# Four rows per partition, spread in place and stored as one 64 KB run: an RMSNorm that repeats its rows

## The chip, the cores and the metric

The kernel runs on one core of one Trainium2 chip. The metric is the device time of one execution in microseconds; the profile is one execution on the same core.

## The reference

```python
# x: (8, 512, 2048) float32, gamma: (2048,) float32
def reference(x, gamma):
    x_rep = np.repeat(x, 2, axis=1)
    rms = np.sqrt((x_rep ** 2).mean(axis=-1, keepdims=True) + 1e-6)
    x_norm = x_rep / rms
    return (x_norm * gamma[None, None, :]).astype(np.float32)
```

Each of the 4096 rows of 2048 values is divided by its root mean square, multiplied by gamma, and written twice, one copy after the other. So 33.55 MB (4096 rows of 8 KB) are read, and 67.11 MB are written.

## The kernel before

The rows are cut into 16 tiles of 256. Each of the 128 partitions holds K = 2 neighbouring rows, so a tile's load is 2.10 MB, with 16 KB in one run for each partition.

Loads are issued from SyncE (SP) on line 59, into `x_tile`. On ACT, line 64 squares each of the two rows into `sq_tile` and sums it into one column of `ss`, and line 72 takes the root for both rows at once. On DVE, line 80 takes the reciprocals, line 84 scales each row into `y_tile` (which is `sq_tile` again), and line 87 multiplies both rows by gamma. Then POOL issues two stores on line 90, one for each repetition: each takes the same two rows, and writes them to every second row of the output, so that a run in the output is one row of 8 KB.

The pools `xin` and `sq` have six buffers each. The Tile framework sets the order of the instructions on each engine and the waits between them: a load waits until the scaling of six tiles ago has read `x_tile`, and a square waits until both stores of six tiles ago have read `sq_tile`. Gamma is loaded on line 44, ahead of all x, into one partition, and POOL spreads it over the 128 partitions on line 45.

Of the kernel before, what the change touches and what calls it, by code (L numbers as in the profile page):

```python
# [1 line left out]

# [4 lines left out]


@with_exitstack  # L10
def kernel(
    ctx: ExitStack,
    tc: tile.TileContext,
    x: bass.AP,
    gamma: bass.AP,
    out: bass.AP,
):
    nc = tc.nc
    P = nc.NUM_PARTITIONS

    B, S, D = x.shape
    Bo, So, Do = out.shape
    R = So // S
    assert D == Do and B == Bo and So == S * R
    eps = 1e-6

    x_f = x.rearrange("b s d -> (b s) d")
    N = B * S
    K = 2
    assert N % (P * K) == 0  # L30
    ntiles = N // (P * K)
    x_t = x_f.rearrange("(n p k) d -> n p k d", p=P, k=K)

    out_v = out.rearrange("b (s r) d -> (b s) r d", r=R)
    out_t = out_v.rearrange("(n p k) r d -> n p k r d", p=P, k=K)

    BUFS = 6
    singles = ctx.enter_context(tc.tile_pool(name="singles", bufs=1))
    xin = ctx.enter_context(tc.tile_pool(name="xin", bufs=BUFS))
    sq = ctx.enter_context(tc.tile_pool(name="sq", bufs=BUFS))  # L40
    small = ctx.enter_context(tc.tile_pool(name="small", bufs=8))

    gamma_b = singles.tile([P, D], mybir.dt.float32)
    nc.sync.dma_start(out=gamma_b[0:1, :], in_=gamma.partition_broadcast(1))
    nc.gpsimd.partition_broadcast(out_ap=gamma_b[:], in_ap=gamma_b[0:1, :])  # L45
    gamma_kd = bass.AP(
        tensor=gamma_b.tensor,
        offset=gamma_b.offset,
        ap=[gamma_b.ap[0], [0, K], gamma_b.ap[1]],
    )  # L50

    eps_t = singles.tile([P, 1], mybir.dt.float32)
    nc.vector.memset(eps_t, eps)  # L53

    inv_d = 1.0 / float(D)

    for i in range(ntiles):
        x_tile = xin.tile([P, K, D], mybir.dt.float32, name="x_tile")
        nc.sync.dma_start(out=x_tile[:], in_=x_t[i])

        sq_tile = sq.tile([P, K, D], mybir.dt.float32, name="sq_tile")
        ss = small.tile([P, K], mybir.dt.float32, name="ss")
        for k in range(K):
            nc.scalar.activation(  # L64
                out=sq_tile[:, k, :],
                in_=x_tile[:, k, :],
                func=mybir.ActivationFunctionType.Square,
                accum_out=ss[:, k : k + 1],
            )

        rms = small.tile([P, K], mybir.dt.float32, name="rms")
        nc.scalar.activation(  # L72
            out=rms[:],
            in_=ss[:],
            func=mybir.ActivationFunctionType.Sqrt,
            scale=inv_d,
            bias=eps_t[:],
        )
        rstd = small.tile([P, K], mybir.dt.float32, name="rstd")
        nc.vector.reciprocal(out=rstd[:], in_=rms[:])  # L80

        y_tile = sq_tile
        for k in range(K):
            nc.vector.tensor_scalar_mul(  # L84
                out=y_tile[:, k, :], in0=x_tile[:, k, :], scalar1=rstd[:, k : k + 1]
            )
        nc.vector.tensor_mul(out=y_tile[:], in0=y_tile[:], in1=gamma_kd)  # L87

        for r in range(R):
            nc.gpsimd.dma_start(out=out_t[i, :, :, r, :], in_=y_tile[:])  # L90


# [1 line left out]
_INS = ['x', 'gamma']  # L94
_OUTS = [((8, 1024, 2048), 'float32')]


# [23 lines left out]
```

## Time and profile before

| | |
|---|---|
| median of 9 runs | 245.0 us (244.92 to 245.18) |
| the profiled execution | 245.1 us, with a span of 243.2 us |
| DVE, ACT, POOL busy | 112.6, 69.5, 29.3 us |
| HBM read, written | 33.56 MB, 67.11 MB |
| store, issue to landing | 40.5 us at the median, 32 stores of 2048 KB |
| load, issue to landing | 24.5 us at the median, 16 loads of 2048 KB |

The span runs from the first instruction of the program to the last; the time of an execution has 1.9 us around it. Below, a group's row gives the line, the engine and the operation, then its busy time and the mean duration of one, and then the idle time of the engine ahead of it with what ended it. In the timeline and the chain, a row starts with its start and its duration in microseconds. The rows of the slices cut the span into 40 equal parts of 6.08 us.

### The profile page before, as it was taken

To read this page: it belongs to the slowest core of one execution; us is meant where nothing else is said; L and a number is where in the kernel's file an instruction comes from. 1 tells how busy PE (TensorE), PEld (TensorE's weight loads), DVE (VectorE), ACT (ScalarE), POOL (GpSimd) and SP (SyncE) were. 2 spreads that over 40 slices of the span, in tenths; PEclk is the share of its full clock that TensorE was granted. 3 is DMA by queue.
4 is the path that set the end of the run, shared out by engine and by line. 5 is a ranking of instruction groups with operands and counts; after the bars stand their busy time and mean duration, and the time that the engine had idled before them with its cause. 6 is when DMAs were issued, how large, how long until landed. Compare 5 with 4: busy or idle time off the path is not lost.

```text
span 243.2 us, 320 instructions
## 1 busy us (share of the span) xinstructions
DVE 112.6 (46%) x65; ACT 69.5 (29%) x82; POOL 29.3 (12%) x37
## 2 busy tenths in 40 slices
DVE  0069999950900049690095709587595600000000
ACT  2598666006000150600615060642624000000000
POOL 4003223411010101110120111111121111000000
DMA  6999999999999999999999999999999999999993
GB/s 220 431 431 431 406 427 430 433 425 431 426 427 435 427 423 429 431 439 422 426 429 438 415 429 430 427 429 429 429 420 425 416 420 419 426 419 425 418 425 148
DMA packets 11012, 100.69 MB, mean 414 GB/s; under 512 B 769, under 2 KB 769, under 8 KB 769
## 3 DMA queue, kind: packets, MB, share of 16 engines
q0 software_dynamic: 8704, 67.11, 65.6%
q1 hardware_dynamic: 2306, 33.56, 32.8%
q14 instruction: 2, 0.02, 0.0%
HBM read 33.56 MB, written 67.11 MB: 414 GB/s over the span
## 4 chain that ended last, share of the span: by engine, by line
DMA 50%; another core or an unknown queue 15%; issue 4%; ACT 3%; DVE 2%; POOL 1%; POOLq 0%; ACTq 0%
DMA out_dram<-sq_tile 50%; ACT sq_tile L64 3%; DVE sq_tile L87 2%; POOL out_dram L90 1%; POOLq L116 0%; ACT rms L72 0%; DVE rstd L80 0%; ACTq L64 0%; POOLq L90 0%
## 5 line engine op out<-in xcount | busy, mean ns | idle before, releaser
L64 ACT ACTIVATE sq_tile<-x_tile 128x2048 f32<-128x2048 f32 x32 | 60.8, 1901 | 114.4 <-DMA out_dram<-sq_tile 101.2
L87 DVE TENSOR_TENSOR sq_tile<-sq_tile,gamma_b 128x4096 f32<-128x4096 f32 x16 | 70.8, 4422 | 0.5
L90 POOL DMA_DIRECT2D out_dram<-sq_tile x32 | 26.8, 839 | 170.3 <-DMA out_dram<-sq_tile 126.6
L84 DVE TENSOR_SCALAR sq_tile<-x_tile,rstd 128x2048 f32<-128x2048 f32 x32 | 40.0, 1293 | 0.5
L80 DVE RECIPROCAL rstd<-rms 128x2 f32<-128x2 f32 x16 | 2.6, 163 | 78.1 <-ACT rms L72 78.1
L64 ACT ACTIVATION_READ_ACCUMULATOR sq_tile<-x_tile 128x1 f32 x32 | 6.0, 186 | 0.0
L72 ACT ACTIVATE rms<-ss,eps_t 128x2 f32<-128x2 f32 x16 | 4.7, 295 | 0.5
L45 POOL PARTITION_BROADCAST gamma_b<-gamma_b x1 | 2.3, 2293 | 2.2 <-DMA gamma_b<-in_gamma_dram 2.2
L64 ACT ACT_TABLE_LOAD x1 | 1.3, 1283 | 0.7 <-PEq L105 0.7
L72 ACT ACT_TABLE_LOAD x1 | 1.3, 1283 | 0.0
L53 DVE MEMSET eps_t<- 128x1 f32 x1 | 0.1, 59 | 0.8 <-PEq L105 0.8
L105 POOL MEMSET const-float32-0.0<- 128x1 f32 x1 | 0.1, 100 | 0.2 <-issue 0.2
L105 POOL MEMSET const-bfloat16-1.0<- 128x1 bf16 x1 | 0.1, 102 | 0.0
L105 POOL MEMSET const-uint8-127<- 128x1 uint8 x1 | 0.1, 102 | 0.0
L105 POOL MEMSET const-float32-1.0<- 128x1 f32 x1 | 0.1, 98 | 0.0
## 6 DMA issues: line engine op xcount, KB each, us to landing
out_dram<-sq_tile POOLq DMA_DIRECT2D x32, 2048.0 KB, 40.5
x_tile<-in_x_dram SPq DMA_DIRECT2D x16, 2048.0 KB, 24.5
gamma_b<-in_gamma_dram SPq DMA_DIRECT2D x1, 8.0 KB
```

The lines of the kernel that those rows point to most:

```text
L45: nc.gpsimd.partition_broadcast(out_ap=gamma_b[:], in_ap=gamma_b[0:1, :])
L53: nc.vector.memset(eps_t, eps)
L64: nc.scalar.activation(out=sq_tile[:, k, :], in_=x_tile[:, k, :], func=mybir.ActivationFunctionType.Square, accum_out=ss[:, k : k + 1],)
L72: nc.scalar.activation(out=rms[:], in_=ss[:], func=mybir.ActivationFunctionType.Sqrt, scale=inv_d, bias=eps_t[:],)
L80: nc.vector.reciprocal(out=rstd[:], in_=rms[:])
L84: nc.vector.tensor_scalar_mul(out=y_tile[:, k, :], in0=x_tile[:, k, :], scalar1=rstd[:, k : k + 1])
L87: nc.vector.tensor_mul(out=y_tile[:], in0=y_tile[:], in1=gamma_kd)
L90: nc.gpsimd.dma_start(out=out_t[i, :, :, r, :], in_=y_tile[:])
L105: nc = _bacc.Bacc("TRN2", target_bir_lowering=False, num_devices=1)
```

## The change

A tile now has K = 4 rows per partition, so there are 8 tiles. Input and output share one buffer `y` of eight rows (64 KB per partition), of which there are three. A load of 4.19 MB puts the four rows of x into the last four slots. Row k of x, in slot 4 + k, is scaled and multiplied by gamma in one DVE instruction into slot 2k, and copied from there to slot 2k + 1: by ACT for the first three rows, and by DVE for the fourth, whose second copy lands on the row of x itself. When all eight slots are filled, ACT issues one store of 8.39 MB, in which each partition is one run of 64 KB. The squares go to a PSUM tile that nobody reads; only their sum is used.

Loads 0 to 2 are issued from SP at the start, the first in four parts of one row each; later loads are issued from SP when their buffer is free. Gamma's load is issued from ACT.

```diff
-    K = 2
+    K = 4
...
-    out_t = out_v.rearrange("(n p k) r d -> n p k r d", p=P, k=K)
+    out_t = out.rearrange("b s d -> (b s) d").rearrange("(n p j) d -> n p (j d)", p=P, j=K * R)
...
-    BUFS = 6
-    xin = ctx.enter_context(tc.tile_pool(name="xin", bufs=BUFS))
-    sq = ctx.enter_context(tc.tile_pool(name="sq", bufs=BUFS))
+    rows = ctx.enter_context(tc.tile_pool(name="rows", bufs=3))
+    junk = ctx.enter_context(tc.tile_pool(name="junk", bufs=1, space=bass.MemoryType.PSUM))
...
+    def load(i, parts=1):
+        y = rows.tile([P, K * R, D], f32, name="y")
+        step = K // parts
+        for k in range(0, K, step):
+            at = K * (R - 1) + k
+            nc.sync.dma_start(out=y[:, at : at + step, :], in_=x_t[i, :, k : k + step, :])
+        ys.append(y)
+    load(0, parts=K)
...
-    nc.sync.dma_start(out=gamma_b[0:1, :], in_=gamma.partition_broadcast(1))
+    nc.scalar.dma_start(out=gamma_b[0:1, :], in_=gamma.partition_broadcast(1))
...
+    load(1)
+    load(2)
...
     for i in range(ntiles):
+        y = ys[i]
         for k in range(K):
+            xk = y[:, K * (R - 1) + k, :]
+            y0, y1 = y[:, R * k, :], y[:, R * k + 1, :]
+            sq = junk.tile([P, D], f32, name="sq")
+            ss = small.tile([P, 1], f32, name="ss")
+            nc.scalar.activation(out=sq[:], in_=xk, func=Act.Square, accum_out=ss[:])
+            rms = small.tile([P, 1], f32, name="rms")
+            nc.scalar.activation(out=rms[:], in_=ss[:], func=Act.Sqrt, scale=inv_d, bias=eps_t[:])
+            rstd = small.tile([P, 1], f32, name="rstd")
+            nc.vector.reciprocal(out=rstd[:], in_=rms[:])
+            nc.vector.scalar_tensor_tensor(
+                out=y0, in0=xk, scalar=rstd[:], in1=gamma_b[:],
+                op0=Alu.mult, op1=Alu.mult,
+            )
+            if k == K - 1:
+                nc.vector.tensor_copy(out=y1, in_=y0)
+            else:
+                nc.scalar.copy(out=y1, in_=y0)
-        for r in range(R):
-            nc.gpsimd.dma_start(out=out_t[i, :, :, r, :], in_=y_tile[:])
+        nc.scalar.dma_start(out=out_t[i], in_=y.rearrange("p j d -> p (j d)"))
+        if i >= 1 and i + 2 < ntiles:
+            load(i + 2)
```

More of the change, by code (lines that the diff above doesn't have):

```diff
@@ L19 @@
     P = nc.NUM_PARTITIONS
+    f32 = mybir.dt.float32
+    Act = mybir.ActivationFunctionType
+    Alu = mybir.AluOpType
     B, S, D = x.shape
@@ L23 @@
     R = So // S
-    assert D == Do and B == Bo and So == S * R
+    assert R == 2 and D == Do and B == Bo and So == S * R
     eps = 1e-6
-    x_f = x.rearrange("b s d -> (b s) d")
+    inv_d = 1.0 / float(D)
+    K = 4
     N = B * S
-    K = 2
     assert N % (P * K) == 0
     ntiles = N // (P * K)
-    x_t = x_f.rearrange("(n p k) d -> n p k d", p=P, k=K)
-    out_v = out.rearrange("b (s r) d -> (b s) r d", r=R)
-    out_t = out_v.rearrange("(n p k) r d -> n p k r d", p=P, k=K)
-    BUFS = 6
+    x_t = x.rearrange("b s d -> (b s) d").rearrange("(n p k) d -> n p k d", p=P, k=K)
@@ L38 @@
+    out_t = out.rearrange("b s d -> (b s) d").rearrange("(n p j) d -> n p (j d)", p=P, j=K * R)
     singles = ctx.enter_context(tc.tile_pool(name="singles", bufs=1))
-    xin = ctx.enter_context(tc.tile_pool(name="xin", bufs=BUFS))
-    sq = ctx.enter_context(tc.tile_pool(name="sq", bufs=BUFS))
+    rows = ctx.enter_context(tc.tile_pool(name="rows", bufs=3))
+    junk = ctx.enter_context(tc.tile_pool(name="junk", bufs=1, space=bass.MemoryType.PSUM))
     small = ctx.enter_context(tc.tile_pool(name="small", bufs=8))
-    gamma_b = singles.tile([P, D], mybir.dt.float32)
@@ L44 @@
-    nc.sync.dma_start(out=gamma_b[0:1, :], in_=gamma.partition_broadcast(1))
-    nc.gpsimd.partition_broadcast(out_ap=gamma_b[:], in_ap=gamma_b[0:1, :])
[L46 to L52, printed above, removed]
+    ys = []
+    def load(i, parts=1):
[5 more added lines that the diff above has]
+        ys.append(y)
@@ L53 @@
+    load(0, parts=K)
+    gamma_b = singles.tile([P, D], f32, name="gamma_b")
+    nc.scalar.dma_start(out=gamma_b[0:1, :], in_=gamma.partition_broadcast(1))
+    nc.gpsimd.partition_broadcast(out_ap=gamma_b[:], in_ap=gamma_b[0:1, :])
+    eps_t = singles.tile([P, 1], f32, name="eps_t")
     nc.vector.memset(eps_t, eps)
-    inv_d = 1.0 / float(D)
+    load(1)
+    load(2)
     for i in range(ntiles):
[L58 to L62, printed above, removed]
+        y = ys[i]
@@ L63 @@
         for k in range(K):
[L64 to L68, printed above, removed]
-            )
[L71 to L87, printed above, removed]
-        for r in range(R):
-            nc.gpsimd.dma_start(out=out_t[i, :, :, r, :], in_=y_tile[:])
+            xk = y[:, K * (R - 1) + k, :]
```

## The prediction

> **What bounds the kernel now.** I read the DMA rows of the slices first, because a kernel that only moves and scales rows is most likely bound there.
>
> ```profile
> span 243.2 us, 320 instructions
> DVE 112.6 (46%) x65; ACT 69.5 (29%) x82; POOL 29.3 (12%) x37
> DMA  6999999999999999999999999999999999999993
> GB/s 220 431 431 431 406 427 430 433 425 431 426 427 435 427 423 429 431 439 422 426 429 438 415 429 430 427 429 429 429 420 425 416 420 419 426 419 425 418 425 148
> HBM read 33.56 MB, written 67.11 MB: 414 GB/s over the span
> ```
>
> The 16 DMA engines are full in 38 of 40 slices while DVE, the busiest engine, works 46% of the span. So time is bytes over rate, plus the two ends, plus any hole in the DMA row; there is no hole. The GB/s row also has two levels: 431 where only loads run (slices 2 to 4), and a mean of 421 in the last nine full slices, where only stores run.
>
> Next the groups and the waits, for durations and to see who waits for whom.
>
> ```profile
> L64 ACT ACTIVATE sq_tile<-x_tile 128x2048 f32<-128x2048 f32 x32 | 60.8, 1901 | 114.4 <-DMA out_dram<-sq_tile 101.2
> L87 DVE TENSOR_TENSOR sq_tile<-sq_tile,gamma_b 128x4096 f32<-128x4096 f32 x16 | 70.8, 4422 | 0.5
> L84 DVE TENSOR_SCALAR sq_tile<-x_tile,rstd 128x2048 f32<-128x2048 f32 x32 | 40.0, 1293 | 0.5
> L72 ACT ACTIVATE rms<-ss,eps_t 128x2 f32<-128x2 f32 x16 | 4.7, 295 | 0.5
> ```
>
> ACT idles 101.2 us for stores to free a buffer: computing has slack, and its waits cost nothing as long as other transfers are queued. Six buffers keep some queued.
>
> Last, the timeline and the chain in order of time, for how two queues share the DMA engines:
>
> ```profile
> 18.65 1.91 ACT L64 ACTIVATE sq_tile<-x_tile 128x2048 f32<-128x2048 f32 x1 [0.15 <-DMA x_tile<-in_x_dram]
> 23.55 1.91 ACT L64 ACTIVATE sq_tile<-x_tile 128x2048 f32<-128x2048 f32 x1 [0.68 <-DMA x_tile<-in_x_dram]
> ...
> 29.96 1.91 ACT L64 ACTIVATE sq_tile<-x_tile 128x2048 f32<-128x2048 f32 x1 [2.18 <-DMA x_tile<-in_x_dram]
> 37.58 1.91 ACT L64 ACTIVATE sq_tile<-x_tile 128x2048 f32<-128x2048 f32 x1 [3.39 <-DMA x_tile<-in_x_dram]
> ```
>
> ```profile
> 56.01 3.90 ACT sq_tile L64 x4
> 84.04 3.90 ACT sq_tile L64 x4
> ```
>
> Alone, 2.10 MB loads land 4.90 us apart (428 GB/s). Beside stores they land 7.62 us apart (275 GB/s). The two starts at 56.01 and 84.04 each waited for one tile's two stores, so 4.19 MB of stores took 28.03 us (150 GB/s). Loads thus get 1.84 times what stores get. A load moves 16 KB per run (two rows) and a store 8 KB per run (one row): near one run each in turn.
>
> **What the Trainium skill says.** DMA: Bandwidth & Descriptors, section Queues, rings and completion order: each DMA engine goes round its queues and drains one packet before switching. The 1.84 agrees with a packet being one run here. The same page, section Issuing engines are not separate DMA queues: all issuers share the 16 engines, so moving stores from POOL to ACT adds no bandwidth by itself; the trace has loads and stores together at 427 to 433, no more than loads alone. The same page, section Where 436 GB/s comes from, puts the ceiling at 435.2 GB/s; the windowed loads at 6 to 9 us show 437, which agrees.
>
> **The change, part by part.** The bytes stay 33.55 MB in and 67.11 MB out.
>
> *Larger runs.* A 16 KB load run takes 4.90/8 = 0.612 us on its engine (8 runs per engine and load); an 8 KB store run at 421 GB/s takes 0.311. That is 0.301 per 8 KB plus 0.010 fixed. A 32 KB run then takes 1.21 us (432 GB/s) and a 64 KB run 2.42 (434). With tile 0's 8 KB load runs I take 432. Bounds: no gain, 424.7 (before's mean, below), and the ceiling of 435.2. Data time 233.0 us (231.3 to 237.0).
>
> *Ends.* Before: the first load is issued at 1.12 and lands at 8.88; less 4.90 of transfer and an estimated 0.5 for landing, data flows from 3.5. It ends near 240.5, so 237.0 us carry 100.66 MB at 424.7 GB/s. After it 2.7 us follow in the span, and 1.9 outside it (245.1 profiled run against a span of 243.2). 3.5+237.0+2.7+1.9 = 245.1, beside a median of 245.0. After: x is issued ahead of gamma, which moves to ACT's queue; data flows from 3.0 (-0.5, bounds -1 to 0). The end is taken as unchanged.
>
> *Computing per tile of four rows.* ACT: 4 squares at 2.0 with their accumulator read (8.88 to 12.79 for two), 4 square roots at 0.30, 3 copies at 1.89 (price: ScalarE: Activation LUTs, What ACT_TABLE_LOAD costs, 186 ns + 0.833 ns per element; the L64 row has the same size at 1.90): 14.9 us. DVE: 4 fused multiplications at 2.3 (half of L87 is 2.21; VectorE: DVE Perf Modes, Side-by-side, gives 2.29 for 2048 elements at one per cycle), 4 reciprocals at 0.17, one copy at 1.25 (as L84): 11.1 us. Both lie beside the 29.1 us that a tile's DMA takes, so their totals cost nothing; what would show is the wait between them, and that sits in the next part. The squares' output going to PSUM has no row; I take the same 1.9 (1.7 to 2.1), covered likewise. POOL's 32 DMA issues (26.8 us) go, from an idle engine: nothing. The 8 store issues on ACT (0.33 each as SP's) are covered too.
>
> *The new waits.* There are now three buffers and one buffer per tile for input and output. Load i+1 (SP) waits for store i-2 to have landed, and nothing is queued behind it but later loads. On ACT, the built order for i from 2 on is: first square of tile i+1, its root, second square, then store i. DVE also runs the reciprocal of tile i+1 before the last copy of tile i. So **store i is queued behind load i+1**, and is issued 2x2.0+0.3+0.1 = 4.4 us after that load lands; from issue to flowing data I take 1.9 us (an estimate: 1.12 to 3.5 above is 2.4 for the first load of all; 1.2 to 2.5 as bounds).
>
> Whether that costs anything depends on the sharing. A store of 8.39 MB has eight 64 KB runs per engine, a load of 4.19 MB eight 32 KB runs. One run in turn gives the load a third: a load (9.7 us alone) and a store (19.4 alone) that start together end together, 29.1 us later. Followed through with 432 GB/s:
>
> - Row 0 lands at 6.0; tile 0 needs 16.2 us of ACT with its table load and 2.5 of the last row's wait: store 0 is issued at 24.7. Loads 0 to 2 keep the DMA busy beyond that.
> - Store 0 has landed at 52.1 and load 3 is issued; store 1 came at 50.1. Hole 0.4.
> - They share and end at 80.6 and 81.6. Load 4 is issued at 80.6, flows at 82.5: hole 1.4. Store 2 comes at 86.0.
> - Store 2 ends at 112.1, load 5 shares with store 3 (issued 105.7) until 140 to 141: hole 1.2. Period 59.5 for two tiles.
> - Store 4 ends at 171.6, load 7 shares with store 5 to 199.5 and 200.7. No load is left; store 6 waits for tile 7's squares, is issued at 205.1, flows at 207: hole 6.8.
> - Stores 6 and 7 take 38.9 more; landed at 246.4.
>
> Sum of holes 9.8. Total: 3.0 + 233.0 + 9.8 + 2.7 + 1.9 = **250.4**: against the profiled 245.1 it is -0.5 - 4.0 + 9.8 = +5.3. The sizes of the holes move by about 1.5 when a copy or the issue time moves by its bounds; the last stays at 6 to 7.
>
> **Rivals.**
>
> *Loads keep at least half (faster).* If a 64 KB run is cut into packets of at most 32 KB, load 7 lands near 190, store 6 is issued at 195, before store 5 ends at 198, and every hole closes: 3.0+233.0+2.7+1.9 = 240.6 (239.0 to 244.6 over the rates). For it: no row of the profile has a run over 16 KB. Against: loads and stores that shared by length of run at 8 and 16 KB. The side decides at a store share near 1.2 times the load's, where the holes are worth 4.2 to 4.5; from about 1.3 they cost 7.2 (247.8), and at 1.6 they are at their full size. Chance 0.22.
>
> *The holes without the rate (slower by more).* The 424.7 stays, because it was never the run's length: 3.0+237.0+9.8+4.6 = 254.4. The two levels 431 and 421 speak against it, since nothing else that the profile shows separates them, except read from write. Inside the likeliest case's range.
>
> *Gain and holes cancel.* Within 0.2% (0.5 us, about what a measurement of this kernel can tell from no change) only if the share falls just at 1.2. Chance 0.03.
>
> *The change doesn't do what it says*: the fused product could be slower than its price and make the ACT-DVE order the bound. The rows leave room: a tile would have to take over 29 us against 14.9 and 11.1. I leave it inside the range.
>
> **How the numbers follow.** Likeliest (0.75): slower, 250.4, own range 247.5 to 254.4. Faster 0.22, same 0.03. Eight in ten needs part of the faster case too: 240.0 to 254.0.
>
> **What would show it.** Right: dips of the DMA row near 81, 141 and, longest, 200 to 207 us; load and store landing together; ACT's first square of tile 7 waiting for load 7 to about 200; the GB/s row near 432 in full slices. Wrong: no dips after the first slice and loads landing some 22 us after issue instead of 29 (sharing by halves); or a full DMA row at 420 (no gain from long runs).

## The result, and the profile after

The changed kernel takes 250.33 us (median of 10 runs, 249.37 to 252.4) against 245.0 before: 1.0221 times as long, with a 95% interval of 1.0207 to 1.0235. The prediction was 250.4. Ratios, here and below, leave out executions more than 1.5% above the fastest one of the same kernel; that touches e5_store_first alone.

The page of the changed kernel, its slices first:

```profile
span 248.4 us, 297 instructions
DVE 88.5 (36%) x73; ACT 115.8 (47%) x122; POOL 2.5 (1%) x5
DMA  7999999999799899798998899999989937797993
GB/s 266 468 438 433 343 496 427 422 422 496 343 427 417 338 343 508 338 507 380 464 496 348 359 401 339 422 507 443 443 380 422 507 169 338 338 507 338 507 507 169
HBM read 33.56 MB, written 67.11 MB: 405 GB/s over the span
```

The DMA row, solid before, now has dips: the deepest in slices 33 and 34 (a 3 and a 7, from 199 to 211 us), others are smaller, one of them near 81 us. The GB/s row jumps between 338 and 508 because a 64 KB run is counted where it starts, and only two or three of them start on each engine in a slice of 6.2 us. Single slices of both rows say little now; a 7 or an 8 may be only that. So one sign that the prediction named, a GB/s row near 432 in full slices, cannot be read off. Longer windows show it: over the last 36 us, where only stores run, the rate is 437 (stretch, its length, busy time of DVE, ACT and POOL, clock, DMA share, GB/s):

```profile
209.00:245.00 36.00, 9.12 (x8) 9.96 (x10) 0.00 (x0) 1.00 1.01 437
```

Groups and waits of the same kernel:

```profile
L71 ACT ACTIVATE sq<-y 128x2048 f32<-128x2048 f32 x32 | 59.7, 1866 | 91.6 <-DMA y<-in_x_dram 89.3
L76 DVE SCALAR_TENSOR_TENSOR y<-y,rstd,gamma_b 128x2048 f32<-128x2048 f32 x32 | 75.2, 2350 | 1.0
L83 ACT COPY y<-y 128x2048 f32<-128x2048 f32 x24 | 44.7, 1890 | 10.2 <-DVE y L76 10.2
L81 DVE COPY y<-y 128x2048 f32<-128x2048 f32 x8 | 9.7, 1214 | 0.1
```

ACT's idle time has changed its cause. Before, it waited 101.2 us for stores to free a buffer, with loaded tiles in hand. Now it waits 89.3 us for loads.

The end of that story, in the chain in order of time and in the timeline:

```profile
174.59 28.91 DMA y<-in_x_dram
203.50 0.02 issue
203.53 2.01 ACT sq L71 x2
```

```profile
203.53 1.88 ACT L71 ACTIVATE sq<-y 128x2048 f32<-128x2048 f32 x1 [25.13 <-DMA y<-in_x_dram]
205.76 1.86 ACT L71 ACTIVATE sq<-y 128x2048 f32<-128x2048 f32 x1
205.97 1.21 DVE L81 COPY y<-y 128x2048 f32<-128x2048 f32 x1
207.21 0.34 ACTq L84 DMA_DIRECT2D out_dram<-y  x1
```

Load 7 is issued at 174.59 and lands 28.91 us later. Then come tile 7's first square on ACT and its first reciprocal on DVE; behind that reciprocal DVE makes the last copy of tile 6 (205.97 to 207.18), and behind the start of tile 7's second square ACT issues store 6, at 207.21. So tile 6, which had long been ready but for one copy, stood behind tile 7 on both engines, and the copy was what came last. Stores 2 to 5 show the same order. The windows show what lies in between:

```profile
202.00:203.00 1.00, 0.00 (x0) 0.00 (x0) 0.00 (x0) 1.00 0.01 0
203.00:209.00 6.00, 3.11 (x3) 4.19 (x5) 0.00 (x0) 1.00 0.41 175
```

**An account of the span.** The trace has a record, with start and duration, for every run that a DMA engine moves. From these I made an account per engine (sums over all engines, divided by 16). "Runs" is each run at its median duration; "stretched" is what runs took beyond that; "empty" is time from 3 us to the last byte in which engines had no run; "rest" is what is left of the span: the start and the end, less the time in which a run starts before the one ahead of it on its engine has ended. Counted where more than 16 runs are open at once, this overlap is 2.2 us before and 0.6 after.

| us | runs | stretched | empty | rest | span |
|---|---|---|---|---|---|
| before | 236.4 | 2.5 | 1.3 | 3.0 | 243.2 |
| after | 232.6 | 5.3 | 7.5 | 3.0 | 248.4 |

So the longer runs bring 3.8, empty engines cost 6.2 more and stretched runs 2.8 more: +5.2. Of the 3.8, some 1.7 had been overlap of short runs, so that they cost no time before; the equal "rest" hides this, because both ends of the span are shorter after.

### The profile page after: what moved, and what is told of

The parts are those of the page before. It is cut to its first block, busy times and chain, and to the rows that moved or that the text cites. A ratio compares the mean times of both kernels' runs of the same rounds, so it can differ in the third digit from the quotient of the medians.

```text
span 248.4 us, 297 instructions
## 1 busy us (share of the span) xinstructions
DVE 88.5 (36%) x73; ACT 115.8 (47%) x122; POOL 2.5 (1%) x5
## 4 chain that ended last, share of the span: by engine, by line
DMA 72%; ACT 11%; DVE 4%; SPq 1%; issue 1%
DMA y<-in_x_dram 44%; DMA out_dram<-y 28%; ACT sq L71 7%; ACT y L83 3%; DVE y L76 3%; DVE y L81 1%; SPq L52 1%; ACT rms L73 1%; DVE rstd L75 0%
## 5 line engine op out<-in xcount | busy, mean ns | idle before, releaser
L71 ACT ACTIVATE sq<-y 128x2048 f32<-128x2048 f32 x32 | 59.7, 1866 | 91.6 <-DMA y<-in_x_dram 89.3
L76 DVE SCALAR_TENSOR_TENSOR y<-y,rstd,gamma_b 128x2048 f32<-128x2048 f32 x32 | 75.2, 2350 | 1.0
L75 DVE RECIPROCAL rstd<-rms 128x1 f32<-128x1 f32 x32 | 5.2, 161 | 132.9 <-ACT rms L73 132.9
L83 ACT COPY y<-y 128x2048 f32<-128x2048 f32 x24 | 44.7, 1890 | 10.2 <-DVE y L76 10.2
L81 DVE COPY y<-y 128x2048 f32<-128x2048 f32 x8 | 9.7, 1214 | 0.1
L73 ACT ACTIVATE rms<-ss,eps_t 128x1 f32<-128x1 f32 x32 | 9.4, 292 | 0.5
L71 ACT ACTIVATION_READ_ACCUMULATOR sq<-y 128x1 f32 x32 | 6.0, 186 | 0.0
```

Source lines behind the costliest of these rows:

```text
L71: nc.scalar.activation(out=sq[:], in_=xk, func=Act.Square, accum_out=ss[:])
L73: nc.scalar.activation(out=rms[:], in_=ss[:], func=Act.Sqrt, scale=inv_d, bias=eps_t[:])
L76: nc.vector.scalar_tensor_tensor(out=y0, in0=xk, scalar=rstd[:], in1=gamma_b[:], op0=Alu.mult, op1=Alu.mult,)
L81: nc.vector.tensor_copy(out=y1, in_=y0)
L83: nc.scalar.copy(out=y1, in_=y0)
```

## The experiments

Each kernel is the changed one with a small edit, except where said. The spans and accounts of all are in a table at the end of this section.

**e1_store32: the store cut into two 32 KB runs**

```diff
-        nc.scalar.dma_start(out=out_t[i], in_=y.rearrange("p j d -> p (j d)"))
+        h = K * R // 2
+        last = nc.scalar.dma_start(out=out_t[i, :, h * D :], in_=y[:, h:, :].rearrange("p j d -> p (j d)"))
+        with tc.issue_after(last.ins):
+            nc.scalar.dma_start(out=out_t[i, :, : h * D], in_=y[:, :h, :].rearrange("p j d -> p (j d)"))
```

> Each store is cut into two of 32 KB runs, issued one behind the other at the place of the one store; loads stay at 32 KB runs, and buffers, engines and order stay. Theory (sharing by run, with store i queued behind load i+1): the load now gets half, lands some 22 us after its issue instead of 29, well ahead of the store beside it, and no hole is left: 241 us (240 to 243). Rival A (three buffers are too few, or ACT's chain through a tile is the bound): nothing changes, 249 to 251. Rival B (a 64 KB run is slow in itself): also faster, but with the holes of the changed kernel still there at 80, 140 and 200 us.

Measured: 248.99 us, 1.0166 (1.0149 to 1.0183). A miss of 8 us. The hole at 203 us did go (empty 2.5 instead of 7.5), but stretched runs rose from 5.3 to 8.4. The share was near what was expected: from 182 to 200 us, while both ran, loads moved 224 GB/s and stores 195. What failed is the step from sharing to time. Load 4 took 26.1 us from issue (82.16) to landing (108.27), not 22, so store 3 was issued at 112.0, when store 2 was about to land (113.5). Each store still waits for the next load, and so is issued only when the store queue has run empty, or nearly so; from 80 us on no load is running then either, and the next load is issued 1.2 to 1.8 us after the store. In the five stretches of 5 to 10 us after such starts (from 25, 80, 115, 145 and 175 us) runs were stretched by 5.3 us in all. In the last four these are store runs and the first runs of the new load, 4 to 7 us after the store was issued. The number touches rival A's range, 249 to 251; e5_store_first and f1_first_store32, with the same three buffers and the same work on ACT, rule that rival out.

**e3_store32_load16: the ratio 1 to 2 again, at half the lengths**

```diff
-        for k in range(0, K, step):
+        for k in (range(0, K, step) if parts == K else reversed(range(0, K, step))):
...
-            load(i + 2)
+            load(i + 2, parts=2)
```

with the store as in e1_store32, and parts=2 for loads 1 and 2 as well.

> As the run before (stores of 32 KB runs), but each load from tile 1 on is cut into two of 16 KB runs, rows 2 and 3 first, so that rows 0 and 1, which the first squares need, land last. The ratio of runs is 1 to 2 again, at half the lengths. Theory: the holes return, longest near 203 us with 6 to 7 us; 252.5 us (250 to 254). Rival B (length, not ratio): as fast as the run before, 240 to 243. Rival A: 249 to 251 in both.

Measured: 249.97 us, 1.0205 (1.0189 to 1.022), just under the expected 250 to 254 and 2.5 below the point. The holes came back where they were expected: slices 33 and 34 (199 to 211 us) show 6 and 5 in the DMA row of this kernel.

```profile
span 248.3 us, 323 instructions
DMA  7999999999999999999999999999999965999995
```

From 178 to 200 us loads moved 143 GB/s and stores 290. So it is the ratio of the runs, not the 64 KB, that makes load 7 and store 5 end together. The time is only 1.0 us above e1_store32, because that one pays in stretched runs instead.

**e5_store_first: the order alone**

```diff
+            with ExitStack() as behind:
+                if k == 0 and store is not None:
+                    behind.enter_context(tc.issue_after(store.ins))
+                nc.scalar.activation(out=sq[:], in_=xk, func=Act.Square, accum_out=ss[:])
...
+        store = nc.scalar.dma_start(out=out_t[i], in_=y.rearrange("p j d -> p (j d)"))
```

This keeps the next tile's first square behind the store on ACT. The last copy on DVE then comes ahead of the next reciprocal too.

> Runs of 64 and 32 KB as in the changed kernel, and the same three buffers; only the first square of tile i+1 is kept behind store i on ACT, so no store waits for the next load. Theory: holes at 80, 140 and 200 us vanish, though ACT idles more at the end of each tile; one hole of up to 3 us may stand ahead of the last store near 217: 242 us (239.5 to 244). Rival A (ACT's chain is the bound): slower than the changed kernel, over 251. Rival that the sharing alone matters, whatever the order: 249 to 251.

Measured: 0.9887 of before (0.9867 to 0.9907), from two executions of 242.1 and 242.4 us, which are as expected to within 0.5 us; the other two took 246.5 and 250.6 (the median of all four is 244.46). The trace kept is that of the fastest, so what lengthened two of them is not known, and the 8 us that are gone of the 250.3 rest on the two faster ones. f1_first_store32 below repeats the step, with 32 KB store runs and with executions that agree. Empty falls to 3.0, all near 218 us, where tile 7 is finished only after store 6 has been sent; stretched falls to 1.8.

**e4_k2_six: six small buffers instead of three large ones**

```diff
-    K = 4
+    K = 2
...
-    rows = ctx.enter_context(tc.tile_pool(name="rows", bufs=3))
+    rows = ctx.enter_context(tc.tile_pool(name="rows", bufs=6))
```

with loads five tiles ahead.

> K = 2 rows per partition and six buffers of 32 KB, everything else as in the changed kernel: loads of 16 KB runs, stores of 32 KB runs, ratio 1 to 2 as there. Theory: with five tiles of loads ahead the store never waits for a load that shares with it, so no hole, and the longer runs' rate shows: 242 us (240.5 to 243.5). Rival (sharing alone costs time, whatever the depth): 249 to 253. Rival (longer runs bring no rate): 245 to 246.

Measured: 249.35 us, 1.0169 (1.0134 to 1.0204). A miss of 7 us, and a number inside the first rival's range. Depth was no cure here, but the trace shows a reason that none of the theories had: the 16 engines did not stay together. The time between the first and the last engine's completion of one load grew from 0.7 us at the start to 12.3 us at 216 us, and the last two engines made up 7.9 of that. A load has landed only when the slowest engine is through. So store 14 waited for load 15 (landed 215.55, store issued 219.25), and in the end two engines worked alone, as the windows show:

```profile
214.00:221.00 7.00, 3.06 (x3) 4.19 (x5) 0.00 (x0) 1.00 0.67 290
236.00:240.00 4.00, 0.00 (x0) 0.00 (x0) 0.00 (x0) 1.00 0.82 352
240.00:247.00 7.00, 0.00 (x0) 0.00 (x0) 0.00 (x0) 1.00 0.10 42
```

**f1_first_store32: e1_store32 and e5_store_first together**

> Two 32 KB-run stores per tile (as in e1_store32) with the first square of the next tile kept behind them (as in e5_store_first). New theory, after the cut alone left 249 us: a store queued behind the next load costs in two ways, as a hole where no transfer is left, and, where a load is still running, as a restart: the store queue has run empty, and when it starts anew beside a load, packets of all 16 engines stretch for about 1 us. With the order changed the store queue never runs empty after the first store, so neither is left: 240 us (239 to 242). Rival (32 KB runs in both queues disturb each other whatever the order): the stretched packets stay as in e1_store32, 245 to 248.

Measured: 240.45 us, 0.981 (0.9796 to 0.9823), from five executions of 239.9 to 240.7 us, where e1_store32 had four of 248.6 to 249.3. The time is as expected. Against e1_store32 only the order differs, and the same stretch of both kernels shows the difference (e1_store32, then f1_first_store32):

```profile
80.00:92.00 12.00, 7.53 (x6) 10.25 (x11) 0.00 (x0) 1.00 0.95 364
143.00:154.00 11.00, 7.49 (x6) 9.25 (x11) 0.00 (x0) 1.00 0.99 382
```

```profile
80.00:92.00 12.00, 8.97 (x8) 10.00 (x10) 0.00 (x0) 1.00 1.01 437
143.00:154.00 11.00, 6.17 (x5) 6.07 (x6) 0.00 (x0) 1.00 0.99 429
```

In e1_store32 the engines count as busy (0.99) at 382 GB/s: a stretched run is busy time that moves too little. A busy row alone would have hidden it. One part of the theory does not fit: in e1_store32, from 80 us on, no load was running at these starts. In both kernels loads 4 to 7 join running stores at 86 to 88, 115 to 119, 144 to 150 and 173 to 181 us. Behind a store queue that had just started anew (e1_store32) runs stretch; behind one that had kept running (f1_first_store32) none does.

**s1_sp_only: one queue for loads and stores**

```diff
-        nc.scalar.dma_start(out=out_t[i], in_=y.rearrange("p j d -> p (j d)"))
+        nc.sync.dma_start(out=out_t[i], in_=y.rearrange("p j d -> p (j d)"))
```

> The changed kernel with its stores issued from SP too, so that one queue carries loads and stores in turn and nothing is shared. The built order then also puts the last copy of a tile ahead of the next tile's first square from tile 2 on. Theory: no sharing and no restart beside a load, the queue always holds a store or a load: 240 us (239 to 243). Rival (a load queued behind a whole store in the one queue arrives too late for its tile): holes of several us per tile, 255 to 280.

Measured: 240.74 us, 0.9827 (0.9813 to 0.984). As expected. The changed runs, buffers and engines are all fine with a single queue. One thing did not fit: runs were stretched by 1.2 us at 25 to 35 us here too, where the first store follows loads in the same queue, and by 0.8 at 160 to 170. So a second queue is not needed for that.

**f3_first_k2: e4_k2_six with the order of e5_store_first**

> e4_k2_six (K = 2, six buffers) with the first square of the next tile kept behind the store. In e4_k2_six two of the 16 DMA engines fell back by 0.7 us per tile, to some 7 us, and each store waited for the next load. Theory: the hole of 3 us near 217 goes, while the two slow engines still end 6 us after the rest: 246 us (244.5 to 247.5). Rival (the slow engines are a result of the order): 240 to 242.

Measured: 248.23 us, 1.0151 (1.0108 to 1.0195), 0.7 above the expected range. The hole near 217 is gone, and the slow engines are not:

```profile
214.00:221.00 7.00, 4.94 (x4) 6.00 (x7) 0.00 (x0) 1.00 1.03 445
234.00:238.00 4.00, 0.00 (x0) 0.00 (x0) 0.00 (x0) 1.00 0.67 287
238.00:245.00 7.00, 0.00 (x0) 0.00 (x0) 0.00 (x0) 1.00 0.10 42
```

So the engines' falling apart is not a result of the order. Its cause was not found.

**e6_before_act: the kernel before, its stores issued from ACT**

```diff
-            nc.gpsimd.dma_start(out=out_t[i, :, :, r, :], in_=y_tile[:])
+            nc.scalar.dma_start(out=out_t[i, :, :, r, :], in_=y_tile[:])
```

> The kernel before with its stores issued from ACT instead of POOL; runs of 16 and 8 KB, six buffers, all else as before. Theory (who issues a store does not matter by itself, and with six buffers the load behind which a store is queued has long landed): 245 us (243.5 to 246.5). Rival (the move from POOL to ACT is itself a cost, through ACT's order): 247 or more. Rival (it is a gain): under 243.

Measured: 241.97 us, 0.9872 (0.9858 to 0.9885). A miss: the move is worth 3.0 us with runs, buffers and loads as they were. It changes more than the issuer's name, though. Each store now stands in ACT's order, and the pages list the stores in a queue of another kind (before, then e6_before_act):

```profile
q0 software_dynamic: 8704, 67.11, 65.6%
```

```profile
q10 hardware_dynamic: 8704, 67.11, 66.1%
```

Which of these brings the 3.0 was not separated. Its rows:

```profile
span 240.1 us, 302 instructions
GB/s 220 434 437 434 382 446 413 438 424 427 437 422 437 435 418 427 442 418 442 415 431 435 433 426 419 430 426 426 433 426 428 428 424 433 426 428 431 422 429 292
```

The last nine full slices have a mean of 428 instead of 421 with the same 8 KB runs. After the last byte 1.3 us follow in the span instead of 2.5. In the account, stretched and empty time are each 0.9 less; before, the empty time is nearly all in the last 3 us, where the last 16 runs end within 1.2 us of each other instead of 0.6.

**g1_first_pool: f1_first_store32 with its stores issued from POOL**

> f1_first_store32 with the stores issued from POOL; ACT has no store in its stream, and on DVE the next tile's first reciprocal is kept behind the last copy, so that no store waits for the next load. e6_before_act had shown the move from POOL to ACT to be worth 3.0 us at 8 KB runs: 1.2 at the end of the span after the last byte, the rest in packets. Theory (the issuer's part is the same at 32 KB runs, less its per-packet share): 242 us (241 to 243.5). Rival (the issuer's part came from the many short runs alone): 240.5. Rival (POOL's stores are late for another reason): over 244.

Measured: 241.03 us, 0.9844 (0.9823 to 0.9864). The issuer, with the queue and the order that go with it, is worth 0.6 us with 32 KB runs, not 3.0 as with 8 KB ones; the result lies between theory and first rival, nearer to the rival. The account shows 1.1 us empty against 0.3, and the end after the last byte 1.9 against 1.4.

**e2_load16: each load in two halves, the needed one first**

```diff
-            load(i + 2)
+            load(i + 2, parts=2)
```

and parts=2 for loads 1 and 2.

> The changed kernel with each load from tile 1 on cut into two, rows 0 and 1 first (16 KB runs), the 64 KB store and the order kept. Store i still stands behind the first two squares of tile i+1, but these now need only the first half of that load. Theory: the wait shortens by half a load, the long hole near 203 us shrinks to about 2 us, restarts beside a load stay (some 3 us): 245 us (242.5 to 247). Rival (the load's smaller share, a fifth, makes it later still): 250 or more.

Measured: 247.42 us, 1.0096 (1.0064 to 1.0128), 0.4 above the range. The hole shrank as expected (empty 1.9), but stretched runs rose to 7.4, and here too engines fell apart, by up to 15 us within one load. A shorter wait helps less than taking the wait away.

**All accounts together**

| us | runs | stretched | empty | rest | span |
|---|---|---|---|---|---|
| after | 232.6 | 5.3 | 7.5 | 3.0 | 248.4 |
| e1_store32 | 233.1 | 8.4 | 2.5 | 2.8 | 246.8 |
| e3_store32_load16 | 233.6 | 5.8 | 6.2 | 2.7 | 248.3 |
| e2_load16 | 233.1 | 7.4 | 1.9 | 2.7 | 245.1 |
| e5_store_first | 232.6 | 1.8 | 3.0 | 2.9 | 240.3 |
| f1_first_store32 | 233.1 | 1.8 | 0.3 | 2.9 | 238.1 |
| g1_first_pool | 233.1 | 1.7 | 1.1 | 3.2 | 239.1 |
| s1_sp_only | 232.6 | 2.9 | 0.5 | 3.0 | 239.0 |
| e4_k2_six | 233.5 | 3.6 | 8.2 | 2.7 | 248.0 |
| f3_first_k2 | 233.5 | 3.0 | 6.9 | 2.7 | 246.1 |
| e6_before_act | 236.4 | 1.6 | 0.4 | 1.7 | 240.1 |

The best of them, f1_first_store32, is also faster than the kernel before.

## Why the prediction was right, and where it was not

**Sharing by run: right.** Load and store rates while both run, from the trace's records of runs:

| kernel | run of load, of store | stretch, us | load, store GB/s |
|---|---|---|---|
| before | 16, 8 KB | 27 to 80 | 279, 149 |
| after | 32, 64 KB | 57 to 79 | 147, 286 |
| e1_store32 | 32, 32 KB | 182 to 200 | 224, 195 |
| e3_store32_load16 | 16, 32 KB | 178 to 200 | 143, 290 |
| e4_k2_six | 16, 32 KB | 100 to 140 | 142, 286 |

One run in turn holds in every pairing to within 15%. The order of starts shows the turn itself: in the changed kernel, from 60 to 75 us, 16 load runs start, then 16 store runs, then 16 load runs, every 3.6 us, which is one run of each (1.21 and 2.42). The Trainium skill (DMA: Bandwidth & Descriptors, section Queues, rings and completion order) has the turn at a packet, of some 9 to 17 descriptors; here it was one run, of 8 to 64 KB.

**Store i behind load i+1: right, and the heart of it.** The table sets the predicted times beside those of the trace.

| event, us | predicted | trace |
|---|---|---|
| store 0 issued | 24.7 | 24.1 |
| store 1 landed | 80.6 | 81.1 |
| store 2 issued | 86.0 | 86.0 |
| store 2 landed | 112.1 | 114.0 |
| load 7 issued | 171.6 | 174.6 |
| load 7 landed | 200.7 | 203.5 |
| store 6 issued | 205.1 | 207.2 |
| store 7 landed | 246.4 | 247.3 |

One detail was off: the prediction let the store wait for both squares, 4.4 us after the load; in the trace it follows 3.7 us after, and DVE's copy behind the reciprocal ends last.

e5_store_first removes this wait alone, on ACT and DVE together, and takes 242.1 to 242.4 in the two executions that are compared. No run tells the order on ACT from that on DVE. The four kernels with K = 4, loads in 32 KB runs and stores on ACT form a square: with the wait 250.3 (64 KB stores) and 249.0 (two of 32 KB), without it 242.3 and 240.5. The order is worth 8.1 to 8.5 us, the sharing 1.3 to 1.8; the 8.5 has executions that agree on both sides.

**The first rival's arithmetic: wrong.** It said that loads with half the rate would close every hole and give 240.6. e1_store32 had the half share and took 249.0. The failed step is "every hole closes" taken for "nothing is lost": with the wait in place the store queue still ran empty or nearly so once per tile, and after each new start runs stretched instead of engines being idle. The prediction had no term for that. f1_first_store32, with the same runs and stretched time down from 8.4 to 1.8, shows that it belongs to the order. What stretches the runs stays open. In most places the store queue had run dry just before and a load was running or soon joined; this is read from where they stand in time and was not isolated, and some 2.6 us of e1_store32's stretched time lie elsewhere, beside 0.5 at the first load.

**The size of the holes: near, with errors that cancelled.** Predicted 9.8. In the trace engines were empty for 7.5, and runs stretched by another 1.5 after the restarts at 80 and 140 us, so 9.0. Two terms in the holes were too long: from issue to the first run it took 1.0 us for load 4 and 0.9 for store 6, which found the engines idle, not 1.9, and the step from a load to the store behind it took 3.7, not 4.4. Not predicted were 3.0 of stretched runs where stores 0, 2 and 4 start beside loads (25, 85, 145 us). On the other side, both ends were shorter than their terms: the first row landed at 5.6, not 6.0, and from the last byte to the end of the span it took 1.4, not 2.7; the runs themselves took 232.6, not 233.0. So +3.0 stands against -0.8, -0.4, -1.3 and -0.4. That the total came within 0.2 us of the profiled 250.2 is luck; the total is better than its parts.

**The gain of longer runs: near in sum, wrong in its cause.** The medians came out as worked out: a 64 KB run takes 2.42 us and a 32 KB run 1.21. But the term of -4.0 laid the whole distance from 424.7 to 432 GB/s to run length, and took the move from POOL to ACT as free. e6_before_act shows 3.0 us from that move with runs unchanged; f1_first_store32 is only 1.5 below that. The prediction read the levels of 431 and 421 as the work of run length, "since nothing else that the profile shows separates them, except read from write". The page does show something else: the loads are in a hardware_dynamic queue and the stores in a software_dynamic one. With the stores in a hardware_dynamic queue the lower level is 428. "Moving stores from POOL to ACT adds no bandwidth by itself" is what failed: the sentence of the skill (same page, Issuing engines are not separate DMA queues) allows for issue time alone, and 3.0 us of 245 with 8 KB runs, 0.6 with 32 KB runs, is what was measured here, the order of the stores having changed with the move.

**The covered work: right.** The fused product took 2.35 us (2.3 used), the copies 1.89 and 1.21 (1.89 and 1.25), the square into PSUM 1.87 (1.9). ACT worked 115.8 us and DVE 88.5 of 248.4, and neither set the end. That ACT's or DVE's order is a bound in another sense, through what is queued behind a wait, is the point above.

## What to carry to other kernels

Where a store is issued by an engine that also computes, look up what stands ahead of it in that engine's order: a store behind the first work of the next tile waits for that tile's load, and with few buffers that load shares the DMA with the store before. The same holds for the engine that makes the store's last piece, here DVE with its copy. In every pairing here, two transfers that shared the engines advanced nearly in proportion to the length of their runs, so lengthening the stores' runs slowed the loads beside them. And count bytes, not busy time, before calling a DMA row full.

## What was not expected of the hardware

- Runs of all 16 engines stretched where stores joined a stream of loads: 32 KB load runs of 1.21 us took 1.9 to 2.3 us once on each engine some 3 us after store 0 was issued in the changed kernel. It was also seen within one queue (s1_sp_only), and where a load joined stores that had just started anew (e1_store32), but not where it joined stores that had kept running (f1_first_store32).
- With 16 KB load runs and 32 KB store runs, both queues never empty and two rows per tile, a few engines fell back by about 0.6 us with every tile, to 8 to 12 us, and the kernel ended on two engines. The kernel before and e6_before_act, with 16 and 8 KB runs, stayed within 2.0 us, f1_first_store32 (32 and 32 KB) within 2.3.
- Issuing stores of 8 KB runs from POOL (a software_dynamic queue) instead of ACT (a hardware_dynamic one) cost 3.0 us, of which 1.2 lay after the last byte; with 32 KB runs it cost 0.6.
